# A pooling stage in which GpSimd takes the subtraction of the token, the small sums of the new rows and the additions to the sums of squares

## The chip, the cores and the metric

The kernel runs on one core of one Trainium2 chip. The metric is the device time of one execution in microseconds (us). The core has five engines with queues of their own: TensorE (PE, with its weight loads as PEld), VectorE (DVE), ScalarE (ACT), GpSimd (POOL) and SyncE (SP, which here only starts loads). Each works its queue off in order, and waits for the others by semaphores.

## The reference

One inference step of a two-layer trunk with 2048 channels in fp32. Layer 0 mixes by two convolutions, layer 1 by pooling over trailing windows; each is followed by a squared-ReLU MLP of 8192 hidden channels. The change lies in layer 1:

```python
def rmsnorm(x, g):
    xf = x.astype(jnp.float32)
    y = xf * lax.rsqrt(jnp.mean(xf * xf, axis=-1, keepdims=True) + EPS)
    return (y * g.astype(jnp.float32)).astype(x.dtype)

def pool_mixer(h, buf, pos, w_groups, scale):
    l = h.shape[1]
    u_ext = jnp.concatenate([buf, h], axis=1)
    cs = jnp.cumsum(u_ext.astype(jnp.float32), axis=1)
    cs = jnp.pad(cs, ((0, 0), (1, 0), (0, 0)))
    end = cs[:, POOL_BUF + 1:]
    hf = h.astype(jnp.float32)
    outs = []
    for g, w in enumerate(POOL_WINDOWS):            # 2, 4, 8, 16
        sl = slice(g * D_POOL, (g + 1) * D_POOL)    # 512 channels
        start = cs[:, POOL_BUF + 1 - w:POOL_BUF + 1 - w + l, sl]
        cnt = jnp.minimum(pos + 1, w).astype(jnp.float32)[None, :, None]
        pooled = (end[..., sl] - start) / cnt - hf[..., sl]
        outs.append(jnp.einsum('nlc,cd->nld', pooled, w_groups[g].astype(jnp.float32)))
    y = jnp.concatenate(outs, axis=-1) * scale.astype(jnp.float32)
    return y.astype(h.dtype), u_ext[:, -POOL_BUF:]

# in the trunk, odd layers
y, npool = pool_mixer(h, bufs_p[o], pos, pool_w[o], pool_scale[o])
x = x + y
x = x + squared_relu_mlp(rmsnorm(x, norm_mlp[layer]), w_mlp_up[layer], w_mlp_down[layer])
```

There is one prompt of 256 rows behind 16 meta rows, and 8 sequences that get 4 new rows each behind 15 kept ones.

## The kernel before

**Layout.** Channels lie on partitions: x is one tile of 128 partitions by 16 channel tiles by 304 columns (272 of the prompt, then 8 x 4 new rows). Each weight is a stream of 128 x 128 tiles in the order of their use. Every fp32 product is made of three matmuls over halves of 12 bits: weights as `wh` and `wl` (L144 on ACT, L145 on DVE, eight tiles per instruction, five such pairs kept), the other operand likewise, in `s0` to `s3` (h and l). `product` (L194) lays out the matmuls of a weight (L219), hands each finished output tile to a function `evac`, and calls hooks at given places, by which a norm is worked out while the tensor engine goes on.

**The order.** The program is written in plain order and a scheduler sets the order of each engine's queue by priorities; splits of weights have a high one. A tile with two buffers makes its third user wait for the first one's readers.

**The pooling stage.** The linear maps are done ahead of the windows, so the four groups of 512 channels, in the order g = 3, 2, 1, 0, each give a z of four channel tiles by 336 columns (304, and 32 of what the kept rows add). ACT evacuates z with the channel scale (L596); with the fourth tile comes `pool_group` (L600): DVE multiplies z by the norm's factor `r` (L604); takes z from the 288 live columns of x (L605); makes the window sums by doubling, g + 1 additions over the prompt's columns (L614); makes those of the new rows, an addition of the kept rows' part (L619) and up to three of shifted z (L624), into the same tile; and adds the sums over w to x, one channel tile at a time (L628). For each such tile `scale_x` (L234) writes the halves that the second MLP multiplies, the upper one on ACT (L239), the lower on DVE (L240), and `square` (L244) adds x * x to a running sum: the square on ACT (L251, two buffers), the addition on DVE (L252).

**What waits for it.** The second MLP's first product takes seven output tiles side by side, channel tile by channel tile in the order in which the groups finish: 21 matmuls per channel tile. Its norm needs the sum of squares of all 16 channel tiles and is started at product 96 of these 112 (`NM_AT`, L264), spread at product 104 (L290), and only then are output tiles evacuated. `new_rows` (L578) makes an output from x as it was, behind the stage.

Of the kernel before, what the change touches and what calls it, by code (L numbers as in the profile page):

```python
# [11 lines left out]
F32 = mybir.dt.float32  # L12
# [4 lines left out]
P = 128  # L17
# [17 lines left out]
# tiles of weights per load, per split, and splits kept  # L35
CT, HT, WB = 16, 8, 5
WARM = 24
# places in the orders below where a norm's sums are taken, and where its result is spread
# [7 lines left out]


def grouped(ks, ms, first):
    """The first `first` output tiles side by side, k outermost; the others one by one."""
    ks, ms = list(ks), list(ms)  # L50
    order = [(k, m) for k in ks for m in ms[:first]]
    return order + [(k, m) for m in ms[first:] for k in ks]


def in_proj_columns():
    """Output tiles of the input projection, so that both mixers get theirs evenly."""
# [33 lines left out]
# columns of the table of per-channel parameters  # L90
# [13 lines left out]
def trunk(  # L104
# [23 lines left out]
    # moving operands: each value as two halves of 12 bits of mantissa  # L128
# [45 lines left out]
    def feed(upto, parts=1):  # L174
        """Halves of the weights, HT tiles at a time."""
# [18 lines left out]
    def product(order, moving, n, evac, n_k, hooks={}, hold=True):  # L194
        """Products of the next tiles of the stream, in `order`; `moving(k)` gives both halves of
        an operand of `n` columns, and `evac(m, psum)` takes each output tile of `n_k` terms, but
        none before the last of `hooks` if `hold`; hooks are called at their places in the order."""
# [36 lines left out]
    def scale_x(m, cols, g0, dst):  # L234
        """Tile m of x times the norm's gain, in halves."""
# [8 lines left out]
    def square(v, s2, first):  # L244
        """Adds v * v to s2."""
# [3 lines left out]
        else:  # L249
            sq = tmp.tile([P, T], F32, tag="sq", name="sq")[:, :n]  # L250
            act.activation(sq, v, AF.Square)  # L251
            dve.tensor_tensor(out=s2[:, :n], in0=s2[:, :n], in1=sq, op=ALU.add)  # L252
# [4 lines left out]
    def rsqrt_mean(sums, n, inv, name):  # L257
        """1 / sqrt(mean + eps) of n columns, from sums over tiles: worked out with the columns on
        partitions, four to a row. Returns a function that puts it on every partition of a bank."""
# [10 lines left out]
        with tc.high_priority():  # L270
# [4 lines left out]
            # one step of Newton's method  # L275
# [19 lines left out]
    def norm_hooks(at, stat, use):  # L295
        """Hooks that work out a norm from product `at[0]` on and put it to use at `at[1]`."""
# [15 lines left out]
    for i in range(WARM):  # L312
        # keeps the tensor engine busy until the first operands are there
        pe.matmul(warm[:, :P], ones, ones, start=True, stop=True)
# [35 lines left out]
    def kept_rows(i):  # L350
        """What the kept rows add to the new ones' convolution."""
# [14 lines left out]
    def mixer_a(i):  # L366
# [21 lines left out]
        for k in range(1, KA):  # L388
            # the rows before the first are zero
# [151 lines left out]
    def pool_state():  # L541
        """What the kept rows add to the windows of the new ones."""
# [57 lines left out]
    def pool_group(g, z):  # L600
# [4 lines left out]
        dve.tensor_tensor(  # L605
            out=x[:, four, live], in0=x[:, four, live], in1=z[:, :, live], op=ALU.subtract
        )
        # sums over the windows, each twice as long as the one before
        src = z
        for step in range(g + 1):  # L610
# [8 lines left out]
        dve.tensor_tensor(  # L619
            out=dst[:, :, TP:], in0=z[:, :, TP:T], in1=z[:, :, T:], op=ALU.add  # L620
        )
        for d in range(1, NS if g else 2):
            o = view(dst[:, 0, :], [[T, 4], [NS, NB], [1, NS - d]], TP + d)
            dve.tensor_tensor(  # L624
                out=o, in0=o, in1=view(z[:, 0, :], [[TE, 4], [NS, NB], [1, NS - d]], TP), op=ALU.add
            )
        for m in range(4 * g, 4 * g + 4):
# [5 lines left out]
            square(x[:, m, live], s2c, m == CHANNELS[1][0])  # L633
# [8 lines left out]
    def rows_out():  # L642
        # off the way of the second MLP's first operands
# [124 lines left out]
```

## Time and profile before

| | before |
|---|---|
| device time, median of 3 runs | 2115.58 us (2114.16 to 2115.6) |
| span of the profiled execution, first to last instruction | 2112.0 us |
| busy: PE / DVE / ACT / POOL | 2093.9 / 1223.4 / 875.7 / 6.3 us |
| matmuls of the pooling maps begin, about | 1244 us |
| sum of squares of the second MLP complete (last L252) | 1316.2 us |
| this MLP's norm begins on PE (L264) | 1318.1 us |

The profiled execution's own time isn't listed apart from its span; the runs' median is 3.6 us above it, and this lies in front of the first and behind the last instruction. Times within the profile are counted from the span's start. A row of a timeline gives the start and the length of one instruction or of some alike, its engine, line, operation, output and inputs, and in brackets how long its engine stood idle before it and for whom. A row of the groups gives count, total busy us, the mean ns of one, and behind the last bar the idle time in front of them. The stage of this change is some 75 of 2112 us.

### The profile page before, as it was taken

What the parts mean: (1) busy time and instruction counts of PE and PEld (TensorE: products, weight loads), DVE (VectorE), ACT (ScalarE), POOL (GpSimd) and SP (SyncE); (2) the same over time, 40 slices, a digit from 0 to 9 for tenths busy, and PEclk for the clock granted to TensorE, in tenths of its full rate; (3) what the DMA queues carried; (4) which work ended last, traced back from release to release, by engine and by line L of the source; (5) the groups of instructions that cost most, each with busy time, mean ns of one, the idle gap of its engine ahead of it and who ended that gap; (6) DMA issues with size and microseconds to landing.
All of it is one profiled execution on the core that took longest, in us unless ns stands there. A gap on an engine that the chain in (4) does not pass through costs nothing.

```text
span 2112.0 us, 35569 instructions
## 1 busy us (share of the span) xinstructions
PE 2093.9 (99%) x15286; PEld 2090.8 (99%) x15286; DVE 1223.4 (58%) x1765; ACT 875.7 (41%) x1181; POOL 6.3 (0%) x32
## 2 busy tenths in 40 slices
PE   9999999999999999999999999999999999999997
PEld 9999999999999999999999999999999999999997
DVE  8999978654444444444444669644454455445454
ACT  7343347443334333433343445533443344334432
POOL 0000000000000000000000000000000000000000
PEclk9999999999999999999999999999999999999999
DMA  7444545444444444444444443544454444444442
GB/s 282 156 157 160 183 164 192 146 159 160 160 160 160 160 155 154 156 156 158 160 160 160 160 140 142 179 166 160 165 174 160 161 170 169 160 163 175 162 161 84
DMA packets 49485, 343.79 MB, mean 163 GB/s; under 512 B 5520, under 2 KB 6560, under 8 KB 8752
## 3 DMA queue, kind: packets, MB, share of 16 engines
q1 hardware_dynamic: 47952, 337.19, 45.6%
q8 instruction: 119, 1.95, 0.4%
q0 software_dynamic: 512, 2.81, 0.3%
q10 hardware_dynamic: 864, 1.53, 0.2%
q14 instruction: 38, 0.31, 0.0%
HBM read 336.33 MB, written 5.17 MB: 162 GB/s over the span
## 4 chain that ended last, share of the span: by engine, by line
PE 96%; DVE 3%; issue 0%; DMA 0%; ACT 0%; SPq 0%; DVEq 0%
PE mm L219 96%; DVE wl L145 1%; DVE win L614 0%; DVE y L661 0%; DMA wt<-w_in 0%; DVE z L604 0%; DVE x L628 0%; DVE x L605 0%; DVE ssum L252 0%; DVE s0l L240 0%; ACT wh L144 0%; DVE s3l L240 0%; DVE win L624 0%; PE nm_r L290 0%; PE nm_mean L264 0%
## 5 line engine op out<-in xcount | busy, mean ns | idle before, releaser
L144 ACT CAST wh<-wt 128x1024 fp32r<-128x1024 f32 (+1 forms) x634 | 662.9, 1047 | 1154.9 <-PE mm L219 1133.2
L145 DVE TENSOR_TENSOR wl<-wt,wh 128x1024 fp32r<-128x1024 f32 (+1 forms) x634 | 773.1, 1221 | 630.3 <-ACT wh L144 629.5
L219 PE MATMUL mm<-s0h,wl 128*128 128x304 f32 (+1 forms) x1472 | 442.3, 301 | 0.3 <-DVE wl L145 0.3
L219 PE MATMUL mm<-s0h,wh 128*128 128x304 f32 (+1 forms) x1472 | 441.0, 300 | 0.0
L219 PE MATMUL mm<-s0l,wh 128*128 128x304 f32 (+1 forms) x1472 | 439.9, 299 | 0.0
L219 PE MATMUL mm<-s1h,wh 128*128 128x304 f32 (+2 forms) x1376 | 413.0, 301 | 1.4 <-ACT s1h L239 1.4
L219 PE MATMUL mm<-s1l,wh 128*128 128x304 f32 (+2 forms) x1376 | 412.1, 300 | 0.1
L219 PE MATMUL mm<-s1h,wl 128*128 128x304 f32 (+2 forms) x1376 | 411.7, 299 | 0.0
L219 PE MATMUL mm<-s2h,wl 128*128 128x304 f32 (+1 forms) x1152 | 345.5, 300 | 0.0
L219 PE MATMUL mm<-s2h,wh 128*128 128x304 f32 (+1 forms) x1152 | 344.6, 299 | 0.0
L219 PE MATMUL mm<-s2l,wh 128*128 128x304 f32 (+1 forms) x1152 | 343.5, 298 | 0.0
L219 PE MATMUL mm<-s3h,wh 128*128 128x304 f32 (+2 forms) x1056 | 315.4, 299 | 2.7 <-ACT z L596 2.7
L219 PE MATMUL mm<-s3l,wh 128*128 128x304 f32 (+2 forms) x1056 | 315.5, 299 | 0.0
L219 PE MATMUL mm<-s3h,wl 128*128 128x304 f32 (+2 forms) x1056 | 314.9, 298 | 0.0
L219 PEld LDWEIGHTS mm<-s0l,wh 128*128 128x128 f32 x1472 | 277.4, 188 | 0.0
L219 PEld LDWEIGHTS mm<-s0h,wl 128*128 128x128 f32 x1472 | 276.4, 188 | 0.5 <-DVE wl L145 0.5
L219 PEld LDWEIGHTS mm<-s0h,wh 128*128 128x128 f32 x1472 | 276.7, 188 | 0.1
L219 PEld LDWEIGHTS mm<-s1h,wh 128*128 128x128 f32 x1376 | 257.9, 188 | 1.7 <-ACT s1h L239 1.7
L219 PEld LDWEIGHTS mm<-s1h,wl 128*128 128x128 f32 x1376 | 258.9, 188 | 0.2
L219 PEld LDWEIGHTS mm<-s1l,wh 128*128 128x128 f32 x1376 | 258.5, 188 | 0.5 <-DVE s1l L240 0.3
L219 PEld LDWEIGHTS mm<-s2l,wh 128*128 128x128 f32 x1152 | 217.0, 188 | 0.1
L219 PEld LDWEIGHTS mm<-s2h,wh 128*128 128x128 f32 x1152 | 216.5, 188 | 0.1
(156 smaller groups left out, 1605.4 us busy)
## 6 DMA issues: line engine op xcount, KB each, us to landing
wt<-w_up SPq DMA_DIRECT2D x128, 1024.0 KB, 4.8
wt<-w_down SPq DMA_DIRECT2D x128, 1024.0 KB, 4.8
wt<-w_in SPq DMA_DIRECT2D x39, 1024.0 KB, 4.8
wt<-w_out SPq DMA_DIRECT2D x16, 1024.0 KB, 4.8
wt<-w_pool SPq DMA_DIRECT2D x4, 1024.0 KB, 4.8
x<-xT SPq DMA_DIRECT2D x3, 608.0 KB, 9.9
o_y<-y ACTq DMA_DIRECT2D x4, 288.0 KB, 2.1
hs<-sa SPq DMA_DIRECT2D x1, 1088.0 KB, 13.0
```

Of the source, the lines that this page charges most:

```text
L144: act.copy(hi, v)
L145: dve.tensor_tensor(out=lo, in0=v, in1=hi.bitcast(F32), op=ALU.subtract)
L219: pe.matmul(acc[m][:, :n], a, b, start=seen[m] == 0 and i == 0, stop=seen[m] == n_k - 1 and i == 2,)
```

## The change

```diff
-    def square(v, s2, first):
+    def square(v, s2, first, by=dve):
...
-            dve.tensor_tensor(out=s2[:, :n], in0=s2[:, :n], in1=sq, op=ALU.add)
+            by.tensor_tensor(out=s2[:, :n], in0=s2[:, :n], in1=sq, op=ALU.add)
...
         dve.tensor_tensor(out=zt, in0=zt, in1=view(r[0], [[0, 4], [1, T]]), op=ALU.mult)
-        dve.tensor_tensor(
+
+        nc.gpsimd.tensor_tensor(
             out=x[:, four, live], in0=x[:, four, live], in1=z[:, :, live], op=ALU.subtract
         )
+        news = pp.tile([P, 4, NB * NS], F32, tag="news", name=f"news{g}")
+        nc.gpsimd.tensor_tensor(out=news, in0=z[:, :, TP:T], in1=z[:, :, T:], op=ALU.add)
+        for d in range(1, NS if g else 2):
+            o = view(news[:, 0, :], [[NB * NS, 4], [NS, NB], [1, NS - d]], d)
+            nc.gpsimd.tensor_tensor(
+                out=o, in0=o, in1=view(z[:, 0, :], [[TE, 4], [NS, NB], [1, NS - d]], TP), op=ALU.add
+            )
...
-        dve.tensor_tensor(
-            out=dst[:, :, TP:], in0=z[:, :, TP:T], in1=z[:, :, T:], op=ALU.add
-        )
-        for d in range(1, NS if g else 2):
-            o = view(dst[:, 0, :], [[T, 4], [NS, NB], [1, NS - d]], TP + d)
-            dve.tensor_tensor(
-                out=o, in0=o, in1=view(z[:, 0, :], [[TE, 4], [NS, NB], [1, NS - d]], TP), op=ALU.add
-            )
+        act.copy(dst[:, :, TP:], news)
         for m in range(4 * g, 4 * g + 4):
...
-            square(x[:, m, live], s2c, m == CHANNELS[1][0])
+            square(x[:, m, live], s2c, m == CHANNELS[1][0], nc.gpsimd)
```

Per group, the subtraction (before L605, now L606) and the sums of the new rows (before L619 and L624, now L610 and L613, in a tile `news` of their own) go to GpSimd; ACT copies `news` into the windows' tile (L627); and for 15 of the stage's 16 squares GpSimd makes the addition. The rest of the diff takes comments out. Line numbers from L604 on shift: window sums L614 become L622, the addition to x L628 becomes L629.

The rows that follow are instructions of a queue in their order, with line, operation, output, inputs and size. First DVE at the beginning of the stage, group 3 (z_12684; wl are the splits of weights), before:

```order
L604 TENSOR_TENSOR z_12684<-z_12684,r_73 128x4x304
L605 TENSOR_TENSOR x<-x,z_12684 128x4x288
L614 TENSOR_TENSOR win_0_12691<-z_12684 128x4x271
L145 TENSOR_TENSOR wl_12677<-wt_12527,wh_12676 128x1024
L614 TENSOR_TENSOR win_1_12693<-win_0_12691 128x4x269
L614 TENSOR_TENSOR win_2_12695<-win_1_12693 128x4x265
L145 TENSOR_TENSOR wl_12755<-wt_12596,wh_12754 128x1024
L614 TENSOR_TENSOR win_3_12697<-win_2_12695 128x4x256
L619 TENSOR_TENSOR win_3_12697<-z_12684 128x4x32
L604 TENSOR_TENSOR z_12738<-z_12738,r_73 128x4x304
```

and now:

```order
L604 TENSOR_TENSOR z_12684<-z_12684,r_73 128x4x304
L622 TENSOR_TENSOR win_0_12696<-z_12684 128x4x271
L622 TENSOR_TENSOR win_1_12698<-win_0_12696 128x4x269
L145 TENSOR_TENSOR wl_12677<-wt_12527,wh_12676 128x1024
L622 TENSOR_TENSOR win_2_12700<-win_1_12698 128x4x265
L622 TENSOR_TENSOR win_3_12702<-win_2_12700 128x4x256
L145 TENSOR_TENSOR wl_12757<-wt_12596,wh_12756 128x1024
L629 SCALAR_TENSOR_TENSOR x<-win_3_12702,x 128x288 x3
L240 SCALAR_TENSOR_TENSOR s3l_3858<-x,pt,s3h_3857 128x288
```

The subtraction and the small sums are gone from between the window sums, and group 3 is added to x ahead of group 2's multiplication by `r`; before, six more rows of group 2 and of small sums stood in front of that.

POOL, whose queue before went straight from the DMA of L546, in layer 0's MLP, to that of L587 behind this stage, now has 33 instructions between them, of which these are the first:

```order
L606 TENSOR_TENSOR x<-x,z_12684 128x4x288
L610 TENSOR_TENSOR news_12691<-z_12684 128x128
L613 TENSOR_TENSOR news_12691<-news_12691,z_12684 128x32x3
L613 TENSOR_TENSOR news_12691<-news_12691,z_12684 128x32x2
L613 TENSOR_TENSOR news_12691<-news_12691,z_12684 128x32
L252 TENSOR_TENSOR ssum<-ssum,sq 128x288
L606 TENSOR_TENSOR x<-x,z_12740 128x4x288
L252 TENSOR_TENSOR ssum<-ssum,sq 128x288
L610 TENSOR_TENSOR news_12790<-z_12740 128x128
L252 TENSOR_TENSOR ssum<-ssum,sq 128x288
```

Additions to the sum of squares now stand between the steps of the next group, in one queue. Then DVE in front of the first lower half of the third group (s1l_100), from the last group's multiplication on, before:

```order
L604 TENSOR_TENSOR z_12942<-z_12942,r_73 128x4x304
L145 TENSOR_TENSOR wl_13025<-wt_12822,wh_13024 128x1024
L145 TENSOR_TENSOR wl_13060<-wt_12923,wh_13059 128x1024
L145 TENSOR_TENSOR wl_13090<-wt_12923,wh_13089 128x1024
L145 TENSOR_TENSOR wl_13118<-wt_13022,wh_13117 128x1024
L145 TENSOR_TENSOR wl_13148<-wt_13022,wh_13147 128x1024
L614 TENSOR_TENSOR win_1_12893<-win_0_12891 128x4x256
L605 TENSOR_TENSOR x<-x,z_12942 128x4x288
L145 TENSOR_TENSOR wl_13176<-wt_13087,wh_13175 128x1024
L628 SCALAR_TENSOR_TENSOR x<-win_1_12893,x 128x288 x3
L145 TENSOR_TENSOR wl_13206<-wt_13087,wh_13205 128x1024
L240 SCALAR_TENSOR_TENSOR s1l_100<-x,pt,s1h_99 128x288
```

and now:

```order
L604 TENSOR_TENSOR z_12948<-z_12948,r_73 128x4x304
L145 TENSOR_TENSOR wl_13033<-wt_12826,wh_13032 128x1024
L240 SCALAR_TENSOR_TENSOR s3l_3852<-x,pt,s3h_3851 128x288
L240 SCALAR_TENSOR_TENSOR s3l_3854<-x,pt,s3h_3853 128x288
L240 SCALAR_TENSOR_TENSOR s3l_3856<-x,pt,s3h_3855 128x288
L145 TENSOR_TENSOR wl_13068<-wt_12929,wh_13067 128x1024
L622 TENSOR_TENSOR win_0_12900<-z_12845 128x4x271
L622 TENSOR_TENSOR win_1_12902<-win_0_12900 128x4x256
L145 TENSOR_TENSOR wl_13098<-wt_12929,wh_13097 128x1024
L629 SCALAR_TENSOR_TENSOR x<-win_1_12902,x 128x288 x4
L145 TENSOR_TENSOR wl_13126<-wt_13030,wh_13125 128x1024
L240 SCALAR_TENSOR_TENSOR s1l_100<-x,pt,s1h_99 128x288
```

wl_13025 of before and wl_13033 of now are the same split, so four splits stand there where seven did; the other three come later. PE's and SP's queues hold the same instructions, with a few matmuls of PE exchanged within a channel tile.

## The prediction

> **What bounds the kernel now.** I read the busy line of the page first, then the waits of TensorE, then the stretch of the pooling stage.
>
> ```profile
> span 2112.0 us, 35569 instructions
> PE 2093.9 (99%) x15286; PEld 2090.8 (99%) x15286; DVE 1223.4 (58%) x1765; ACT 875.7 (41%) x1181; POOL 6.3 (0%) x32
> PE mm L219 <- ACT z L596: 2.7, 1, 2.7
> PE mm L219 <- ACT s1h L239: 1.4, 1, 1.4
> ```
>
> PE is busy for all but 18 us of the span, and the two waits below it (line, what was waited for, total us, times, longest) are the only ones of size between the start and the last norm. Both lie in the stage that is edited. So a change there can win what PE waits there, and no more. How much that is, I read from the starts of PE's matmuls around the gaps.
>
> ```profile
> 1276.43 0.29 PE L219 MATMUL mm<-s3l,wh 128*128 128x288 f32 x1
> 1276.76 0.40 PE L219 MATMUL mm<-s3h,wh 128*128 128x288 f32 x1
> ...
> 1281.09 0.29 PE L219 MATMUL mm<-s3l,wh 128*128 128x288 f32 x1
> 1281.22 0.29 PE L219 MATMUL mm<-s3h,wl 128*128 128x288 f32 x1
> 1284.18 0.40 PE L219 MATMUL mm<-s3h,wh 128*128 128x288 f32 x1 [2.67 <-ACT z L596]
> ...
> 1300.07 0.29 PE L219 MATMUL mm<-s3h,wl 128*128 128x288 f32 x1
> 1301.80 1.19 PE L219 MATMUL mm<-s1h,wh 128*128 128x288 f32 x7 [1.44 <-ACT s1h L239]
> 1303.05 0.40 PE L219 MATMUL mm<-s1l,wh 128*128 128x288 f32 x1
> ```
>
> Undisturbed matmuls of this shape start 0.13 us apart (1281.09 and 1281.22). Against that pace PE loses 0.20 us at 1276.8, 2.83 at 1284.2, 1.60 at 1301.8 and, after the seven matmuls of that row (7 x 0.13), 0.33 at 1303.05: **4.9 us** in all. That is the most the change can save.
>
> What PE waits for is late because of VectorE:
>
> ```profile
> 1254.30:1318.20 63.90, 59.69 (x424) 58.76 (x423) 63.64 (x99) 35.41 (x62) 0.00 (x0) 1.00 0.36 132
> 1318.20:1400.00 81.80, 81.80 (x621) 81.69 (x620) 45.31 (x65) 39.67 (x60) 0.54 (x1) 1.00 0.49 172
> ```
>
> The columns after the length are busy us of PE, PEld, DVE, ACT and POOL, then the clock. From the first window sum to the second MLP's norm DVE works 63.6 of 63.9 us without a gap; ACT has half its time free and GpSimd does nothing. Behind 1318 DVE has room again and PE loses nothing. The granted clock is 1.00 throughout, so no term is due to it.
>
> **What leaves DVE.** The groups of DVE in 1253 to 1320 that the diff takes away (total busy us, mean ns of one), and two rows of DVE's timeline:
>
> ```profile
> L252 DVE TENSOR_TENSOR ssum<-ssum,sq 128x288 f32<-128x288 f32 x15 | 6.8, 451 | 0.0
> L605 DVE TENSOR_TENSOR x<-x,z 128x1152 f32<-128x1152 f32 x4 | 5.4, 1356 | 0.0
> L619 DVE TENSOR_TENSOR win<-z 128x128 f32<-128x128 f32 x4 | 1.1, 285 | 0.0
> L624 DVE TENSOR_TENSOR win<-win,z 128x96 f32<-128x96 f32 x4 | 1.0, 254 | 0.0
> L624 DVE TENSOR_TENSOR win<-win,z 128x64 f32<-128x64 f32 x3 | 0.7, 221 | 0.0
> L624 DVE TENSOR_TENSOR win<-win,z 128x32 f32<-128x32 f32 x3 | 0.6, 216 | 0.0
> ...
> 1301.35 1.23 DVE L145 TENSOR_TENSOR wl<-wt,wh 128x1024 fp32r<-128x1024 f32 x1
> 1302.49 0.51 DVE L240 SCALAR_TENSOR_TENSOR s1l<-x,pt,s1h 128x288 fp32r<-128x288 f32 x1
> ```
>
> The sum is 6.8 + 5.4 + 1.1 + 1.0 + 0.7 + 0.6 = 15.6 us in 33 instructions. DVE starts an instruction before the one ahead is over: the split of the last two rows begins at 1301.35, takes 1.23 and is followed at 1302.49, after 1.14, so 0.08 to 0.09 us overlap. 33 x 0.08 = 2.6 us of the 15.6 are such overlap: DVE's queue gets shorter by **13.0 us**, where 4.9 would do.
>
> **What comes on GpSimd.** The same 33 instructions, with 4 x 1152 + 4 x 128 + (4 x 96 + 3 x 64 + 3 x 32) + 15 x 288 = 10,112 elements per partition. No row shows an addition there. The nearest ones:
>
> ```profile
> L547 POOL MEMSET part<- 128x512 f32 x1 | 0.5, 524 | 59.9 <-DVE s0l L145 59.9
> masks.py:199 POOL TENSOR_SCALAR_AFFINE_SELECT ident<-ident 128x128 f32<-128x128 f32 x1 | 0.3, 283 | 0.0
> L315 POOL MEMSET inv_d<- 128x1 f32 x1 | 0.1, 98 | 0.0
> ```
>
> One element costs 0.098 us, so that is the fixed part. From below: the memset writes 512 elements in 0.524, 0.83 ns each; 33 x 0.098 + 10,112 x 0.83 ns = 11.6 us. The affine select, which reads one operand and writes, has 283/128 = 2.21 ns per element if all of it grows with size, or (283 - 98)/128 = 1.45 behind the fixed part. From above: a second operand at most doubles the latter, 2.9 ns: 32.5 us. I take 0.098 us and 2.21 ns together, a little over the only row that reads and computes, since an addition reads one operand more, and between both ends: 3.2 + 22.4, **25.7 us**. One x - z then is 2.6 us, one addition of squares 0.74.
>
> In the Trainium skill, the GPSIMD Engine Reference (section "Elementwise — side-by-side cycle accounting") gives 4497 ns for an addition of 2048 fp32 elements; by its 2.2 ns each GpSimd's work would be 22.2 us and the forecast below 2115.6 + 22.2 - 13.0 - 2.0 = 2122.8, and no run here shows it.
>
> **Is GpSimd in time, if nothing disturbs it?** The rows that say it, from DVE's timeline and from the groups of DVE and ACT:
>
> ```profile
> 1254.33 1.42 DVE L604 TENSOR_TENSOR z<-z,r 128x1216 f32<-128x1216 f32 x1
> ...
> L614 DVE TENSOR_TENSOR win<-win 128x1060 f32<-128x1060 f32 x1 | 1.3, 1264 | 0.0
> L145 DVE TENSOR_TENSOR wl<-wt,wh 128x1024 fp32r<-128x1024 f32 x19 | 22.9, 1222 | 1.6 <-ACT wh L144 1.5
> ...
> L251 ACT ACTIVATE sq<-x 128x288 f32<-128x288 f32 x15 | 6.5, 436 | 0.1
> L239 ACT ACTIVATE s3h<-x,pt 128x288 fp32r<-128x288 f32 x8 | 4.3, 534 | 0.0
> L575 ACT COPY r<-np_r 128x304 f32<-128x304 f32 x1 | 0.4, 413 | 0.0
> ```
>
> For the first group z is ready at 1254.33 + 1.42 = 1255.75. GpSimd then needs 5 x 0.098 + 1472 x 2.21 ns = 3.7 us for x - z and the four steps of the small sums, so until 1259.5, and the copy on ACT follows. Meanwhile DVE has four window sums and two splits in front of the first instruction that reads either (the order above), 4 x 1.26 + 2 x 1.22 - 6 x 0.08 = 7.0 us, until 1262.8. GpSimd is 3 us early; its price could nearly double.
>
> The additions of squares add a wait: the square on ACT has two buffers, so it now waits for GpSimd's addition of two squares ago, and behind it on ACT's queue stand the upper halves that PE needs. ACT makes a pair (L239 and L251) in 0.53 + 0.44 = 0.97 us at most, some 0.8 with overlap; an addition of 0.74 us keeps step, and with DVE's gaps between groups it catches up. The four copies L627 of 128 columns lie between nothing and the 0.41 us of a copy of 304, at most 1.6 us on an engine with 28 us free; costed at nothing, covered by that idle time. Their in-order wait for GpSimd holds the evacuations of the next group behind them, and that cover lasts as long as the 3 us above. The DMA of L587 moves back on POOL's queue behind the last addition; nobody waits for it before the end, so nothing. SP's queue keeps its order of loads.
>
> **The term that decides.** Every DVE row above reads two SBUF tensors, and so does every instruction that moves. The nearest that the trace has to both engines reading:
>
> ```profile
> 1.52 0.28 POOL masks.py:199 TENSOR_SCALAR_AFFINE_SELECT ident<-ident 128x128 f32<-128x128 f32 x1
> 5.42 0.69 DVE L145 TENSOR_TENSOR wl<-wt,wh 128x512 fp32r<-128x512 f32 x1 [5.42 <-ACT wh L144]
> ```
>
> GpSimd's only instruction that reads is over before DVE's first begins; its other work is memsets, which only write, and issues of DMAs. So no row shows it. The cost is bounded from both sides. If they run side by side, DVE is 13.0 us better off, PE's waits go, and the time falls by 4.9. If one keeps the other from reading, DVE stands still for GpSimd's 25.7 us: its queue grows by 25.7 - 13.0 = **12.7 us**, in a stage where it has no gap to take it. What PE has in hand at the stage's end is read from the last sum of squares and the norm's first matmul:
>
> ```profile
> 1315.71 0.45 DVE L252 TENSOR_TENSOR ssum<-ssum,sq 128x288 f32<-128x288 f32 x1
> 1318.13 0.62 PE L264 MATMUL nm_mean<-inv_d,ssum 128*72 128x1 f32 x8
> ```
>
> 1318.13 - 1316.16 = 2.0 us. PE then starts the norm 12.7 - 2.0 = 10.7 us later than now, and is the bound again from there.
>
> I take the second as the likelier. No row decides it; the choice rests on two things that rows do show: every term is a two-operand read on both sides, over 25.7 of 64 us, and the gain is capped at 4.9 while each us taken from DVE counts in full. With a share f of GpSimd's time taken from DVE, the change is 25.7 f - 13.0 - 2.0, not below -4.9: the whole gain stays up to f = 0.39, and the loss reaches 0.2% (4.2 us) at f = 0.75.
>
> The Trainium skill's page "SBUF — State Buffer", section "Who interferes with whom", says that a DVE instruction with two SBUF inputs contends with a GpSimd instruction that reads SBUF, and that whoever comes second waits for the whole of the other. By that rule f is 1; by the absence of it the time would be 2110.7. No run here shows it.
>
> **The rivals.**
> - **Side by side** (the other side: faster). Decides if f is below 0.39 and GpSimd's price stays under about twice mine. For it: GpSimd is 3 us early and ACT half free. Against: only the missing row. Time 2115.6 - 4.9 = 2110.7.
> - **In between**: f from 0.4 to 0.75, or full exclusion at the lowest price (11.6 - 13.0 - 2.0 = -3.4). 2112 to 2119.8; middle 2116.
> - **GpSimd too slow by itself**: above about 5 us for x - z the copy L627 comes after DVE wants it, and each group adds the excess. At 2.9 ns and 0.098 it is 3.4 us for x - z and 4.8 for the chain, still under 7.0; so at my bounds this doesn't decide. At 5 ns the chain is 7.8 us and four groups lose 0.8 each against a gain of 4.9: 2114. Small.
> - **The change doesn't do what it says**: excluded by the order, where the 33 rows stand on POOL and DVE has none of them.
>
> **How the numbers follow.** The sum is made against the span of 2112.0; the runs' median of 2115.58 is 3.6 us longer, which I keep. Forecast, exclusion: 2115.6 + 10.7 = 2126.3, with a chance of 0.62; its own range goes by the upper price, 32.5 - 13.0 - 2.0 = 17.5, to 2133, and down to 2119.8. Below 10.7 speaks that the order puts three splits of 1.14 us behind what PE needs from the third group, above it each handover between the engines. Side by side 0.20, in between 0.16, GpSimd by itself 0.02. About 0.2% is what a measurement of this kernel tells from no change: faster 0.20, within 0.18, slower 0.62. With 0.20 on the fast side the range has to take it in: 2110 to 2134.
>
> **What would show it.** Right: GpSimd busy 22 to 33 us in the stage; the 19 splits at L145 take more than 1.22 us or stand idle before them, though ACT is done; PE's waits grow to some 15 us; the norm's matmul comes near 1329. Wrong: splits at 1.22 us as before, DVE with gaps, PE without waits, the norm near 1313; then the exclusion is not there. If DVE is undisturbed and PE waits for the copy L627 or for POOL's sums, the price of GpSimd was the error.

## The result, and the profile after

| | before | after |
|---|---|---|
| device time, median of 5 runs on one chip | 2115.22 us (2113.87 to 2115.6) | 2122.24 us (2121.5 to 2123.58) |
| ratio, with its 95% interval | | 1.0033 (1.0022 to 1.0044) |
| span of the profiled execution | 2112.0 us | 2121.8 us |
| norm's first matmul (L264), counted from the matmul `np_r` that ends the norm ahead of the stage | 66.19 us | 71.73 us |
| norm's last matmul (`nm_r`, L290), counted likewise | 70.04 us | 77.77 us |

The kernel is slower by 0.33%, 7.0 us. The ratios, here and at the experiments, leave out single executions that took about twice as long or more, so they aren't quite the quotients of the medians. The profiled execution after is the one of 2123.58 us, the slowest of the five. The one before was faster than its median: wherever both are on record, this kernel's time is 2.0 to 2.1 us above its span, so a span of 2112.0 us means some 2114.1 (of the 3.6 us named ahead of the prediction, only these 2.0 to 2.1 lie in front of the first and behind the last instruction). The two traces therefore differ by 9.8 us, and sums over them come out above 7.0. `np_r` begins at 1251.94 us of the span before and at 1251.77 after.

The busy line of the page after:

```profile
PE 2097.6 (99%) x15286; PEld 2094.1 (99%) x15286; DVE 1230.9 (58%) x1732; ACT 876.7 (41%) x1185; POOL 55.1 (3%) x65
```

VectorE (DVE) has 33 instructions fewer, whose own time was 15.6 us, and is busy 7.5 us longer than its 1223.4 before. GpSimd (POOL) has gained 48.8 us where 25.7 were forecast. So instructions on both engines hold time in which they only stand.

The waits of TensorE (PE) in and behind the stage (line, what was waited for, total us, times, longest):

```profile
PE mm L219 <- ACT z L596: 5.7, 1, 5.7
PE mm L219 <- DVE s1l L240: 2.2, 1, 2.2
PE nm_r L290 <- DVE nm_diag L281: 2.0, 1, 2.0
```

With 0.4 more for s1h they are 10.3 us in place of 4.1, and a new one is at the norm. What ended the wait for z, the longest, was GpSimd: ScalarE may evacuate this z only when the last small sum that reads the old one is done, and that sum stands behind a subtraction and additions of squares in GpSimd's one queue.

```profile
1281.36 1.40 ACT L596 ACTIVATE z<-mm,pt 128x336 f32<-128x336 f32 x3 [6.74 <-POOL news L613]
```

Which instructions of DVE grew, from its groups between 1253 and 1330 us (total busy us, mean ns of one); first after, then the same of before:

```profile
L145 DVE TENSOR_TENSOR wl<-wt,wh 128x1024 fp32r<-128x1024 f32 x20 | 26.6, 1343 | 1.3 <-ACT wh L144 1.3
L240 DVE SCALAR_TENSOR_TENSOR s3l<-x,pt,s3h 128x288 fp32r<-128x288 f32 x8 | 10.8, 1393 | 0.5 <-ACT s3h L239 0.5
L240 DVE SCALAR_TENSOR_TENSOR s1l<-x,pt,s1h 128x288 fp32r<-128x288 f32 x8 | 7.7, 998 | 0.0
L622 DVE TENSOR_TENSOR win<-win 128x1024 f32<-128x1024 f32 x3 | 6.5, 2177 | 0.1
L622 DVE TENSOR_TENSOR win<-win 128x1076 f32<-128x1076 f32 x2 | 5.0, 2514 | 0.0
```

```profile
L145 DVE TENSOR_TENSOR wl<-wt,wh 128x1024 fp32r<-128x1024 f32 x22 | 26.5, 1223 | 3.8 <-ACT wh L144 3.7
L240 DVE SCALAR_TENSOR_TENSOR s3l<-x,pt,s3h 128x288 fp32r<-128x288 f32 x8 | 4.0, 513 | 0.0
L240 DVE SCALAR_TENSOR_TENSOR s1l<-x,pt,s1h 128x288 fp32r<-128x288 f32 x8 | 4.1, 511 | 0.0
L614 DVE TENSOR_TENSOR win<-win 128x1024 f32<-128x1024 f32 x3 | 3.7, 1220 | 0.0
L614 DVE TENSOR_TENSOR win<-win 128x1076 f32<-128x1076 f32 x2 | 2.5, 1274 | 0.0
```

The same instructions on the same sizes take longer: 20 x 0.120 + 8 x 0.880 + 8 x 0.487 + 3 x 0.957 + 2 x 1.240 = 18.7 us, and 1.6 more in the smaller differences of the other window sums, L604 and L629: **20.3 us**. Against the 13.0 us that left DVE's queue it is 7.3 us more work over this window.

How much of it reaches TensorE is read where TensorE waits for DVE last ahead of the norm, at the first lower half of the third group. Its row, and that of the last addition of squares:

```profile
1307.69 0.40 PE L219 MATMUL mm<-s1l,wh 128*128 128x288 f32 x1 [2.24 <-DVE s1l L240]
1319.54 0.81 POOL L252 TENSOR_TENSOR ssum<-ssum,sq 128x288 f32<-128x288 f32 x1 [1.74 <-ACT sq L251]
```

Counted from `np_r`, TensorE starts on this half after 55.92 us, before after 51.11 (1303.05): 4.8 later. From there to the norm it doesn't wait again, and about six matmuls of 0.13 us that lay ahead of this half before now lie behind it; so the norm's first matmul is 71.73 - 66.19 = 5.5 us later. The sum of squares doesn't set it: it is complete at 1320.35, 3.2 us ahead of the norm, where before it was 2.0. On DVE the 4.8 us up to the end of this half are made up of 17.0 us of standing and 0.5 of a gap, less 9.7 of work that left from there and 3.4 for the three splits that now come later, plus 0.4 for an addition to x that comes sooner.

How one instruction stands for another is seen in the timelines, here DVE and then POOL (start, length):

```profile
1270.22 4.91 DVE L240 SCALAR_TENSOR_TENSOR s3l<-x,pt,s3h 128x288 fp32r<-128x288 f32 x3
1270.92 2.91 POOL L606 TENSOR_TENSOR x<-x,z 128x1152 f32<-128x1152 f32 x1
1273.79 1.02 POOL L252 TENSOR_TENSOR ssum<-ssum,sq 128x288 f32<-128x288 f32 x1
```

Three instructions of 0.51 us fill 4.91 us, and GpSimd's subtraction and one of its additions lie inside them.

Between the norm's two matmuls lie 6.0 us now and 3.85 before. Rows of the timelines of PE and DVE:

```profile
1323.50 0.62 PE L264 MATMUL nm_mean<-inv_d,ssum 128*72 128x1 f32 x8
1322.42 4.62 DVE L145 TENSOR_TENSOR wl<-wt,wh 128x1024 fp32r<-128x1024 f32 x4
1326.96 0.15 DVE L272 TENSOR_SCALAR nm<-nm_mean 72x4 f32<-72x4 f32 x1
1329.54 0.72 PE L290 MATMUL nm_r<-nm_diag,ones 72*128 72x288 f32 x2 [2.02 <-DVE nm_diag L281]
```

The mean is there at 1324.1, and the first step of the norm begins at 1326.96, behind four splits in DVE's queue. TensorE gets to `nm_r` 2.0 us too early.

Last, the clock, in windows around TensorE's longest wait and behind `nm_r` (busy us of PE, PEld, DVE, ACT and POOL, then the clock):

```profile
1275.92:1279.33 3.41, 0.37 (x3) 0.14 (x2) 3.41 (x3) 0.00 (x0) 3.33 (x3) 1.00 0.00 0
1279.33:1282.74 3.41, 0.79 (x3) 0.79 (x4) 3.38 (x4) 1.38 (x4) 3.33 (x3) 0.50 0.14 24
1282.74:1286.16 3.42, 3.42 (x16) 3.42 (x15) 3.42 (x2) 1.60 (x4) 3.42 (x2) 0.50 0.73 283
1330.53:1333.94 3.41, 3.41 (x17) 3.41 (x16) 1.89 (x5) 1.38 (x4) 0.00 (x0) 0.50 0.84 310
```

From 1279.3 to 1286.2 the granted clock is 0.50, and matmuls start 0.24 us apart instead of 0.13. By these rows this first fall is no loss of its own, and neither is the longer wait for z: TensorE comes later to the halves s1h and s1l, for which it still waits 0.4 and 2.2 us, and DVE has only one gap, of 0.5 us, that it didn't have before. The second fall has no such wait behind it in the stage; some 14 matmuls at 0.24 us make it about 1.5 us. The two traces' difference is then 5.5 us at the norm's first matmul, 2.2 between its two and 2.3 behind them, less 0.2 by which `np_r` begins sooner: 9.8 us.

### The profile page after: what moved, and what is told of

Same layout as the page of the kernel before. It is cut to its first block, busy times and chain, and to the rows that moved or that the text cites. A ratio compares the mean times of both kernels' runs of the same rounds, so it can differ in the third digit from the quotient of the medians.

```text
span 2121.8 us, 35591 instructions
## 1 busy us (share of the span) xinstructions
PE 2097.6 (99%) x15286; PEld 2094.1 (99%) x15286; DVE 1230.9 (58%) x1732; ACT 876.7 (41%) x1185; POOL 55.1 (3%) x65
## 4 chain that ended last, share of the span: by engine, by line
PE 95%; DVE 2%; issue 1%; POOL 1%; ACT 0%; DMA 0%; SPq 0%; DVEq 0%; POOLq 0%
PE mm L219 95%; DVE wl L145 1%; DVE y L662 0%; POOL news L613 0%; DVE s3l L240 0%; DVE s1l L240 0%; DMA wt<-w_in 0%; DVE win L622 0%; POOL x L606 0%; DVE x L629 0%; ACT wh L144 0%; POOL ssum L252 0%; DVE s0l L240 0%; DVE z L604 0%; POOL news L610 0%
```

## The experiments

The first four were run in 3 rounds, the others in 5, each beside the kernel before on the same chip. The times are medians.

| run | us | before beside it | ratio (95% interval) |
|---|---|---|---|
| 37 additions on scratch, GpSimd | 2134.78 | 2115.77 | 1.0090 (1.0073 to 1.0107) |
| 60 memsets on scratch | 2116.20 | 2115.77 | 1.0001 (0.9991 to 1.0010) |
| 36 copies on scratch | 2124.69 | 2115.77 | 1.0037 (1.0024 to 1.0050) |
| 37 additions on scratch, one stage later | 2115.88 | 2115.77 | 1.0001 (0.9992 to 1.0011) |
| only the squares' additions moved | 2116.13 | 2116.05 | 0.9999 (0.9991 to 1.0008) |
| only the subtraction moved | 2123.26 | 2116.05 | 1.0030 (1.0018 to 1.0043) |
| only the small sums moved | 2113.58 | 2116.05 | 0.9987 (0.9978 to 0.9996) |
| the change without the subtraction | 2118.16 | 2115.95 | 1.0011 (1.0002 to 1.0019) |
| small sums in their own tile, on VectorE | 2116.64 | 2115.95 | 1.0001 (0.9992 to 1.0011) |
| squares last, one subtraction less | 2113.28 | 2116.05 | 0.9988 (0.9979 to 0.9997) |
| squares last alone | 2118.94 | 2115.93 | 1.0015 (1.0005 to 1.0024) |
| squares last, one subtraction less, small sums on GpSimd | 2117.59 | 2115.95 | 1.0008 (0.9999 to 1.0017) |

### Does reading on GpSimd hold VectorE at all?

The theory is that a two-operand instruction of DVE and a reading instruction of GpSimd exclude each other; the rival, that they run side by side and the change's loss comes from handovers. Four kernels add work to GpSimd that nobody needs, on a tile that nobody else uses; the queues of the other engines are those of before. The first has the change's own sizes:

```diff
+    scr = pp.tile([P, 2 * T1], F32, name="scr", bufs=1)
+    nc.gpsimd.memset(scr, 0.0)
+
+    def scratch(rt):
+        group = 2 * [2 * T1] + [128, 96, 64, 32]
+        for n in 3 * (group + [T1] * 4) + group[:4] + [T1] * 3:
+            nc.gpsimd.tensor_tensor(
+                out=scr[:, :n], in0=scr[:, :n], in1=view(rt, [[0, 2], [1, n // 2]]), op=ALU.add
+            )
...
         act.copy(r[0], rn)
+        scratch(r[0])
```

> The kernel before, all of its work on its engines and every queue of PE, DVE and ACT in the same order, and beside it 37 additions of two operands on GpSimd (10,112 elements per partition, as many as the change moves) into a scratch tile that nobody reads, from the pooling norm on. Nothing waits for them, so they can cost time only by being in another engine's way. Exclusion (an instruction of DVE that reads two SBUF tensors and one of GpSimd that reads SBUF keep each other out): DVE's splits and window sums get longer by 22 to 28 us in all, PE waits that much more less 2 us of slack, 2135 to 2145 us. Rival, GpSimd only too slow or too late for those who wait for it: no change, 2113 to 2118, DVE's splits at 1.22 us.

19 us slower, at the lower end of the range (0.2 us under it), with nothing to hand over. Two groups of DVE, 1253 to 1330 us:

```profile
L145 DVE TENSOR_TENSOR wl<-wt,wh 128x1024 fp32r<-128x1024 f32 x15 | 20.1, 1358 | 1.6 <-ACT wh L144 1.5
L252 DVE TENSOR_TENSOR ssum<-ssum,sq 128x288 f32<-128x288 f32 x11 | 6.5, 590 | 0.0
```

The split is at 1358 ns instead of 1223, the addition at 590 instead of 451, though their data have nothing to do with the scratch. Side by side falls.

The second kernel has 60 memsets of 576 columns in the place of the additions (`nc.gpsimd.memset(scr, 0.0)`), the third 36 copies of 288 columns (`nc.gpsimd.tensor_copy(out=scr[:, :T1], in_=scr[:, T1:])`): writes alone, and reads with one operand. (In both, one addition of 32 columns, 0.9 us, goes ahead of them.)

> The kernel before and beside it, in the same place, 60 memsets of 576 columns on GpSimd (some 35 us of work that writes and doesn't read). If reading is what collides: no change, 2113 to 2118, splits at 1.22 us. If any work of GpSimd holds DVE up (writes, too): 30 us more, about 2145.

> The kernel before and beside it, in the same place, 36 copies of 288 columns on GpSimd: 10,368 elements with one operand to read. If any reading of GpSimd excludes a two-operand instruction of DVE: DVE loses GpSimd's whole time in them, 36 times 0.35 to 0.5 us, 12 to 18 us, so 2125 to 2132 us. If only an instruction of GpSimd with two operands collides: no change, 2113 to 2118.

A group of POOL and one of DVE, first with memsets, then with copies:

```profile
L580 POOL MEMSET scr<- 128x576 f32 x60 | 34.8, 580 | 3.5
L145 DVE TENSOR_TENSOR wl<-wt,wh 128x1024 fp32r<-128x1024 f32 x21 | 25.3, 1225 | 4.9 <-ACT wh L144 4.9
```

```profile
L580 POOL COPY scr<-scr 128x288 f32<-128x288 f32 x36 | 35.7, 993 | 2.2
L145 DVE TENSOR_TENSOR wl<-wt,wh 128x1024 fp32r<-128x1024 f32 x19 | 24.0, 1278 | 2.0 <-ACT wh L144 1.9
```

34.8 us of writes leave the split at 1225 ns and the time as it was; copies that keep GpSimd busy as long make it 1278 ns and cost 0.37%, a little less than expected. It is reading that collides, with one operand too.

The fourth puts the same 37 additions behind the second MLP's norm, where DVE has gaps:

```diff
         act.copy(rt[:, :n], rn)
+            if layer:
+                scratch(rt)
```

> The same 37 additions as in the first of these kernels, but from the second MLP's norm on, where DVE is busy for about half of the time. Exclusion with DVE's load as what decides: splits get longer there as well, but PE waits for none of them, 2113 to 2119 us. If the collision costs PE directly, or wherever it happens: 20 us more, 2135 or above.

DVE's groups between 1323 and 1380 us, here and then before:

```profile
L145 DVE TENSOR_TENSOR wl<-wt,wh 128x1024 fp32r<-128x1024 f32 x18 | 26.7, 1483 | 8.9 <-ACT wh L144 8.8
L145 DVE TENSOR_TENSOR s0l<-u,s0h 128x288 fp32r<-128x288 f32 x8 | 7.5, 961 | 0.0
L511 DVE SCALAR_TENSOR_TENSOR a<-mm,r 128x288 f32<-128x288 f32 x15 | 6.4, 450 | 3.5 <-PE mm L219 3.4
```

```profile
L145 DVE TENSOR_TENSOR wl<-wt,wh 128x1024 fp32r<-128x1024 f32 x18 | 22.1, 1225 | 16.4 <-ACT wh L144 16.4
L145 DVE TENSOR_TENSOR s0l<-u,s0h 128x288 fp32r<-128x288 f32 x8 | 3.4, 451 | 0.0
L511 DVE SCALAR_TENSOR_TENSOR a<-mm,r 128x288 f32<-128x288 f32 x15 | 6.6, 455 | 7.3 <-PE mm L219 7.2
```

The collision is there (1483 for 1225 ns, 961 for 451) and costs no time, since the gaps behind the bars shrink from 16.4 to 8.9 us and take it. L511, which has one operand in PSUM, is at 450 ns for 455, though 13 of its 15 instructions here overlap an addition of GpSimd: this instruction of DVE, with a single operand in SBUF, isn't held.

In the Trainium skill, the page "SBUF — State Buffer", section "Who interferes with whom", says that a DVE instruction with two SBUF inputs contends with a GpSimd instruction that reads SBUF, not with one that only writes, and that one with at most one SBUF input, outside the two-port modes, does not. All three are in these rows.

### Which part of the change costs what?

Three kernels keep one part of the change each and give the others back to DVE. For the squares alone, the call `square(..., nc.gpsimd)` stays and the subtraction and the sums are as before; likewise for the others. Theory: each part costs what DVE stands for it minus what leaves it. Rival: ScalarE's copy of the small sums (L627) waits in order for GpSimd and holds the evacuations of z behind it, so the loss is where the copy is.

> Only the 15 additions of squares (4,320 elements) are on GpSimd; the subtractions and the small sums are back on VectorE, and there is no copy of small sums on ScalarE. Theory of exclusion: the additions take 0.8 to 1.0 us each when nothing disturbs them, 12 to 15 us, of which VectorE stands for about three quarters (9 to 11), against 5.6 us that leave it; minus the 2.0 us in hold: 1.5 to 4 us slower than before, 2117 to 2120, splits at L145 above 1.25 us. Rival, the change's loss comes from ScalarE's copy of the small sums, which waits in order for GpSimd: without the copy VectorE only gains, faster, 2110 to 2113, splits at 1.22.

> Only the four subtractions x - z are on GpSimd, 2.9 us each when undisturbed, 11.6 us; 5.1 us leave VectorE, and there is no copy of small sums. Theory of exclusion at three quarters: VectorE is 8.7 - 5.1 = 3.6 us later, minus 2.0 in hold: 1 to 4 us slower than before, 2116.5 to 2120. Rival, the copy is what costs: faster, 2110 to 2113.

> Only the small sums (14 instructions, 1,184 elements, some 7 us on GpSimd undisturbed) are there, with ScalarE's copy of them; 2.3 us leave VectorE. Theory of exclusion at three quarters: 5.1 - 2.3 = 2.8 us later, minus 2.0 in hold: 0 to 2.5 us slower, 2115 to 2118. Rival, the copy is what costs: it is here as in the change, so nearly the whole loss is here, 2119 to 2123, with TensorE waiting 5 us or more for ScalarE's evacuation of z.

The copy is not it: where it is kept, with the small sums, the kernel isn't slower. The squares cost nothing that can be measured, where 1.5 to 4 us were expected. The subtraction alone costs 0.30%, nearly as much as the whole change and some 3 us more than the range expected. Rows of that kernel's timeline at its first, second and fourth subtraction, DVE first, then POOL:

```profile
1257.28 3.66 DVE L615 TENSOR_TENSOR win<-win 128x1076 f32<-128x1076 f32 x1
1268.40 2.72 DVE L625 TENSOR_TENSOR win<-win,z 128x64 f32<-128x64 f32 x1
1306.43 2.90 DVE L240 SCALAR_TENSOR_TENSOR s1l<-x,pt,s1h 128x288 fp32r<-128x288 f32 x1
...
1256.01 3.79 POOL L606 TENSOR_TENSOR x<-x,z 128x1152 f32<-128x1152 f32 x1 [908.38 <-DVE z L604]
1267.26 3.78 POOL L606 TENSOR_TENSOR x<-x,z 128x1152 f32<-128x1152 f32 x1 [7.46 <-DVE z L604]
1303.28 5.74 POOL L606 TENSOR_TENSOR x<-x,z 128x1152 f32<-128x1152 f32 x1 [15.97 <-DVE z L604]
```

DVE stands 3.66 - 1.27 = 2.4, 2.72 - 0.22 = 2.5 and 2.90 - 0.51 = 2.4 us, and about as much at the third; together some 9.5 us for the 5.1 that left its queue, 4.4 more. A subtraction that isn't itself held up takes 2.9 us on GpSimd (2.91 above) and 1.36 on DVE. It also stands in a bad place: at 1268.40 and at the third subtraction the instruction held is the small sum L625 that reads z last, and until that is over ScalarE may not evacuate the next z into its buffer:

```profile
1287.65 0.97 ACT L596 ACTIVATE z<-mm,pt 128x336 f32<-128x336 f32 x2 [7.67 <-DVE win L625]
1288.24 0.61 PE L219 MATMUL mm<-s3h,wh 128*128 128x288 f32 x1 [4.38 <-ACT z L596]
1296.04 4.63 DVE L145 TENSOR_TENSOR wl<-wt,wh 128x1024 fp32r<-128x1024 f32 x4 [2.17 <-ACT wh L144]
```

TensorE waits 4.4 us for the bank that z still holds, and then works on at half clock, as a window shows:

```profile
1290.00:1300.00 10.00, 10.00 (x66) 10.00 (x65) 7.80 (x13) 6.40 (x11) 0.00 (x0) 0.83 0.19 49
```

66 matmuls lie between 1290 and 1300, where the kernel before has 78. Here the clock does cost: DVE, whose splits wait for ScalarE's halves and with them for buffers that TensorE frees, has a gap of 2.2 us at 1296 that it didn't have before. The sum doesn't close, though: the norm's first matmul is 8.8 us later than before in these traces, while 4.4 us of standing less 2.0 in hand would make it 2.4. The rest lies in these gaps and waits as far as the rows show, and was not tried apart.

The squares alone: in the same way of counting, the splits grow by 1.7 us, L240 by 6.0 and a window sum by 0.6; 8.3 us stand against 5.6 that left, and of the 2.7 between them 2.0 are in hand.

For the small sums the expectation by exclusion was missed on the good side. DVE stands 2.2 us and is relieved of 2.3. The 2.5 us between the medians are not seen in its one profiled execution, whose norm begins 66.45 us after `np_r` (before 66.19) and whose span is 2111.8 us (before 2112.0). In both of these traces the clock stays at 1.00 through the stage. The runs without a trace point to the clock: the eleven of this kernel took 2112.66 to 2114.01 us, and of the 28 beside it the four with the highest mean clock, 0.998, took 2114.02 to 2114.6, the others up to 2118.0. Against those four only some 0.5 us are left. TensorE's waits are short and apart in this kernel (1.3, 0.6 and 1.2 us), which fits the last section; the clock inside the other runs is not on record, only its mean. Another way that it could be is the place: the sums are now made ahead of the long window sums, so z is free sooner. That is tried by itself, with the sums in the same tile of their own and the same copy, but on DVE (the shifted additions likewise):

```diff
-        nc.gpsimd.tensor_tensor(out=news, in0=z[:, :, TP:T], in1=z[:, :, T:], op=ALU.add)
+        dve.tensor_tensor(out=news, in0=z[:, :, TP:T], in1=z[:, :, T:], op=ALU.add)
```

> As the small sums alone, with the tile of their own and ScalarE's copy, but the sums on VectorE and nothing on GpSimd. If what the small sums won came from the work taken off VectorE, nothing is won here, 2115.5 to 2117.5. If it came from the place of the sums (z is read for the last time before the long window sums and not behind them, so ScalarE may evacuate the next z sooner), it is won here too, 2113 to 2114.5, with TensorE's wait for z at L596 below 2 us instead of 2.7.

No gain. TensorE's waits:

```profile
PE mm L219 <- ACT s1h L239: 4.7, 1, 4.7
```

The wait for z (2.7 us before) is gone altogether, and the wait for s1h has grown from 1.4 to 4.7: DVE has as much to do as before, and TensorE only arrives earlier at what is late. The wait in one piece then brings the clock down:

```profile
1300.00:1304.00 4.00, 1.76 (x7) 1.66 (x8) 4.00 (x9) 2.64 (x7) 0.00 (x0) 0.50 0.74 262
```

So a sooner z alone is worth nothing, and what the small sums win on GpSimd is by these runs mostly a clock that doesn't fall; that was not tried by itself.

Last the complement, the change with the subtraction given back to DVE. Rival: the parts hurt each other in GpSimd's one queue.

> The change without its subtraction: squares and small sums on GpSimd, x - z back on VectorE. If each part costs VectorE its own standing time and the subtraction is the part that loses, VectorE stands some 8 us for the squares and 2 for the small sums, against 5.6 and 2.3 that leave it, less 2.0 in hold: no change within 2 us, 2114 to 2118. Rival, the loss comes from all three together in one queue (sums that wait on GpSimd behind additions, ScalarE's copy behind both): about half of the change's loss stays, 2118.5 to 2122.

2.2 us slower, 0.2 above the theory's range and 0.3 below the rival's. TensorE at the norm:

```profile
1318.53 0.68 PE L264 MATMUL nm_mean<-inv_d,ssum 128*72 128x1 f32 x8
1324.90 0.72 PE L290 MATMUL nm_r<-nm_diag,ones 72*128 72x288 f32 x2 [2.30 <-DVE nm_diag L281]
```

The norm's first matmul comes 66.54 us after `np_r`, 0.35 later than before, about what DVE's standing gives (10.6 us for 7.9, less 2.0 in hand, is 0.7); the sum of squares ends 66.48 us after `np_r` here, so what was in hand is used up. The 2.3 us at `nm_r` are the rest, and the changed kernel has nearly the same wait, 2.0. So of the change's 7.0 us, 7.0 - 2.2 = 4.8 go with the subtraction, and some 2 with the splits ahead of the norm. That the splits' place costs the 2 us was read from the rows, not tried alone.

### A version that beats both?

What the profile suggests is to relieve DVE without GpSimd. Behind the last group's halves all 16 squares are taken (none is needed sooner), and in the group with a window of two, x - z isn't made: with z' the row before, x + (z + z') / 2 - z = x + (z' - z) / 2.

```diff
-        dve.tensor_tensor(
-            out=x[:, four, live], in0=x[:, four, live], in1=z[:, :, live], op=ALU.subtract
-        )
+        if g:
+            dve.tensor_tensor(
+                out=x[:, four, live], in0=x[:, four, live], in1=z[:, :, live], op=ALU.subtract
+            )
...
+            here, back = src[:, :, lo:TP], src[:, :, lo - d : TP - d]
             dve.tensor_tensor(
-                out=dst[:, :, lo:TP], in0=src[:, :, lo:TP], in1=src[:, :, lo - d : TP - d],
-                op=ALU.add,
+                out=dst[:, :, lo:TP], in0=back, in1=here, op=ALU.add if g else ALU.subtract
             )
...
         dve.tensor_tensor(
-            out=dst[:, :, TP:], in0=z[:, :, TP:T], in1=z[:, :, T:], op=ALU.add
+            out=dst[:, :, TP:], in0=z[:, :, T:], in1=z[:, :, TP:T],
+            op=ALU.add if g else ALU.subtract,
         )
...
-            square(x[:, m, live], s2c, m == CHANNELS[1][0])
+        if g == GROUPS[-1]:
+            for m in CHANNELS[1]:
+                scaled[m] = square(x[:, m, live], s2c, m == CHANNELS[1][0])
```

(`square` here returns its addition, so that `new_rows` is still issued behind the stage.) The second run below has only the last of these edits, the third has all and the small sums as the change has them.

> The kernel before, without GpSimd: all 16 squares of the stage and their additions are put behind the last group's halves, and in the last group (window of two) x - z is left out, since x + (z' - z) / 2, with z' the row before, is the same sum. If the order of VectorE's queue sets TensorE's waits, 12 additions (4.4 us) no longer stand ahead of the third group's halves, and the sum of squares, 1.3 us shorter in all, still ends within the 2.0 us in hold: 2 to 4 us faster than before, 2112 to 2114. Rival: the additions that now stand behind the last halves end later than TensorE's 112 tiles, and what is won in the middle is waited for at the norm: no change, 2115 to 2117.

> As the run with the squares last, but with the subtraction in the last group as in the kernel before; this tells which of its two edits won. If it was the order (the additions out of the way of the third group's halves), most of the 2.8 us is won here too, 2113 to 2114.5. If it was the 1.3 us less work in the last group, or both are needed, since the additions end 1.3 us later here and TensorE waits for the sum of squares, nothing is won, 2115.5 to 2117.

> The squares behind the last group, no subtraction in the last group (both as in the run with the squares last), and the small sums on GpSimd with ScalarE's copy (as in the run of the small sums alone). Each alone won about 2.6 us, and TensorE's waits of the kernel before hold 4.9. If they win at different waits (the bank of z, and the third group's halves), 4 to 5 us faster than before, 2111 to 2112.5; if both win the same one, 2 to 3 us, 2113 to 2114.

The first is 0.12% faster, as expected. With the order alone the kernel is 3.0 us slower than before, which neither theory gave; its wait at the norm's second matmul shows why:

```profile
PE nm_r L290 <- DVE nm_diag L281: 3.4, 1, 3.4
```

What the order wins in the middle is waited for at the end (0.4 us at the norm's first matmul, 3.4 at its second), and behind these waits the clock is at 0.50 from 1325.8 to 1332.6. With the small sums on GpSimd as well, the two gains didn't add; nothing was won. A row of ScalarE's timeline in that kernel:

```profile
1299.21 0.30 ACT L628 COPY win<-news 128x128 f32<-128x128 f32 x1 [6.69 <-POOL news L615]
```

Here the copy does cost, as the rival of the runs by parts had it: DVE's queue has got shorter and wants the small sums sooner, GpSimd's additions stand behind DVE (3.1 us for the first of a group, where the small sums alone took 1.7), and ScalarE, which waits for them in order, makes the third group's halves only behind the copy at 1299.2. TensorE waits 2.2 us for them, until 1300. That this is the whole loss was not tried.

So the best found are two kernels at 0.9987 and 0.9988 of before, less than the 0.2% that counts here as a difference. The stage holds 4.9 us by the trace before, in which the clock doesn't fall, and some 1.4 us more in an execution in which it does (the last section).

## Why the prediction was right

It gave 2126.3, with 2110 to 2134, and slower with a chance of 0.62; 2122.24 was measured. The mechanism was right, and two of its sizes and its end were not. By its steps:

- **What bounds the stage**: right. DVE has no gap there, so what it stands is paid; one stage later the same collision is free.
- **Exclusion rather than side by side**: right, and shown by the additions on scratch, with nothing else changed. The sentence of the Trainium skill's page "SBUF — State Buffer", section "Who interferes with whom", by which f was 1 holds in its kind. In its size not quite: of a subtraction of 2.9 us DVE stood 2.4, of an addition of squares of 0.8 to 1.0 us some 0.55 (8.3 us over 15); where the rest goes, no row shows.
- **The term that was mis-sized is DVE's queue, +12.7 us; +7.3 was measured.** GpSimd's price was too low (2.6 us for a subtraction of 2.9, 0.74 for an addition of 0.81 at the least, and 4.0 for the small sums, which take some 7 at the least lengths seen; 31 us in all where 25.7 were forecast, itself 25.6 by its own terms). The share of it that DVE stands, taken as the whole, was too high: 20.3 us stood, about two thirds. The two errors made up for each other in part.
- **The 2.0 us in hand** were taken off at the wrong place. 7.3 - 2.0 = 5.3 lies near the 5.5 us of the norm's first matmul by luck: TensorE was held not by the sum of squares, which was 3.2 us early, but by the third group's first lower half, 4.8 us late. There the three splits that come later took off 3.4 us, which the forecast names as speaking for less and leaves out of its sum.
- **The end of the stage** was taken as the point from which TensorE is the bound again. It isn't: the backlog of splits stands ahead of the norm's small steps on DVE and costs 2.2 us more up to `nm_r`, and the clock falls once more behind that wait. So that the measured 7.0 us lie as near to the 10.7 forecast as they do is partly luck: a queue that grew less, and an end that cost more.
- **Its signs**: the splits got longer (1343 ns for 1222). GpSimd's 48.8 us lie above the 22 to 33 given, since it stands as well, and TensorE's waits (10.3 us for some 15) and the norm (1323.5 for near 1329) fell short with the queue.
- **ScalarE's copy, costed at nothing with 3 us of cover**: the cover failed, since GpSimd's chain itself stood behind DVE (ScalarE waited 4.0 and 4.4 us for it at two copies, and 6.7 us to evacuate z). Costed at nothing it was still about right for this change: with the small sums alone the copy is there and no time is lost. Where DVE is relieved in other ways as well, the last run shows, it does cost.
- **No term for the clock**: wrong for the changed kernel, where it is at 0.50 for 6.8 us, covered by the next wait, and for 3.4 us behind `nm_r`, not covered. In the kernel with the subtraction alone it costs as well.
- **The unlike parts** were priced in one sum by elements. The runs show that one of three, the subtraction, carries most of the loss.

## What to carry to other kernels

Before work is moved from VectorE to GpSimd, set what GpSimd takes for it against what VectorE saves: where VectorE's instructions read two SBUF tensors and it has no gap, here 2.4 us were paid for each subtraction that had taken 1.28, and the small sums cost as much as they saved (2.2 us for 2.3). Work that came in a stage where VectorE has gaps, or that only wrote, cost nothing. And where one engine bounds a stage, taking away a wait elsewhere lets TensorE only arrive earlier at the next one: look for what shortens the bounding queue, up to the last small step that hangs on it. Several short waits of TensorE can be cheaper than the same time in one piece, because of the clock.

## What the runs showed of the hardware

**TensorE's clock falls after short waits, if they lie badly.** In all five kernels in which TensorE waited 4.4 us or longer in one piece, the granted clock went to 0.50 (the change, the additions and the copies on scratch, the subtraction alone, the small sums in their own tile on VectorE). Shorter waits of 1.7 to 3.4 us did it in about half the cases, and the same wait can go both ways: the one of 2.7 us for z is in the kernel before and in the kernel with the additions one stage later, whose queues are the same up to there. First before, then the other:

```profile
1279.84:1283.25 3.41, 1.68 (x13) 1.44 (x11) 3.41 (x8) 0.00 (x0) 0.00 (x0) 1.00 0.00 0
1283.25:1286.67 3.42, 2.48 (x18) 2.49 (x19) 3.42 (x12) 3.08 (x8) 0.00 (x0) 1.00 0.02 5
```

```profile
1280.34:1283.75 3.41, 1.09 (x9) 0.86 (x7) 3.41 (x10) 0.26 (x1) 0.00 (x0) 1.00 0.00 0
1283.75:1287.17 3.42, 3.08 (x13) 3.08 (x14) 3.42 (x10) 3.42 (x10) 0.00 (x0) 0.50 0.02 5
```

The windows are not chosen freely. In each trace the steps of the clock lie whole multiples of 3.41 us apart (in the change 1279.33, 1286.16, 1330.53 and 1333.94), and these are the windows of that grid. Before, a window's end divides the wait: TensorE is busy for 1.68 us of one and 2.48 of the next, and the clock stays. In the other kernel nearly all of the wait is in one window, busy for 1.09 us, and the clock falls at its end. Over the 14 traces, up to the last norm, the clock fell behind each of the 12 windows at full clock in which TensorE stood for 1.9 us or longer, and behind 2 of the 26 in which it stood for 1.0 to 1.8 (1.73 us with the squares last and one subtraction less, 1.50 with the memsets). This grouping was made afterwards; the two exceptions, and the last norm, behind which it fell after less in some traces, stay open.

In the Trainium skill, the page "TensorE: Matmul & The Clock Gate", section "Part 1: The HAM clock gate", says that half rate comes after an idle window of about 3.4 us that runs freely, so that the moment varies. The grid of 3.41 us and the long waits agree; that a window needn't be idle as a whole, and that somewhat over half of it was enough, is not in that sentence.

Where the grid lies differs from trace to trace (the first step is at 4.2 to 7.2 us). That it also differs between executions of one kernel, and so gives it several times, fits the runs beside the experiments but no trace shows it: the kernel before took 2113.7 to 2114.6 us in those with a mean clock of 0.998 and 2117.4 to 2117.8 in those with 0.995. A fall that no later wait covers cost 1.3 to 1.5 us here (the norm's first matmul comes 66.19 us after `np_r` before, and 67.53 and 67.63 with the additions one stage later and the memsets). That makes a wait of some 2 us dearer or not, and is likely part of why gains of 2 us didn't add.
